# Moving the adaLN loads and the spill and mixer-row stores of a recurrence stage from SyncE's DMA queue to GpSimd's

## The chip, the cores and the metric

The kernel runs on one core of one Trainium2 chip. The metric is the device time of one execution in microseconds (us). The kernel before the change took 2364.33 us in the median of three runs (2362.54 to 2365.67). About 0.2 % (4.7 us) is what a measurement of this kernel can tell from no change.

## The reference

One decoder block on x (512 tokens x 2048 channels, float32), modulated by a vector c:

```python
c_act = silu(c)
mod = c_act @ w_ada + b_ada                  # 6 x 2048: shift, scale, gate, twice
h = rmsnorm(x, norm1_g) * (1 + sc1) + sh1
p = h @ w_in                                 # r, k, v, three low-rank inputs, pool channels
y_rwkv = rwkv7_mixer(p[..., :N_RWKV_COLS])   # 16 heads of 64: a recurrence over 512 tokens
y_pool = pool_mixer(p[..., N_RWKV_COLS:])    # causal means over windows 2, 4, 8, 16
x = x + gt1 * (concat([y_rwkv, y_pool]) @ w_out)
h = rmsnorm(x, norm2_g) * (1 + sc2) + sh2
x = x + gt2 * conv_ffn(h)                    # up 2048 -> 2 x 5632, conv of width 3, gate, down
out = rmsnorm(x, norm_f_g)
```

The recurrence of one head holds a 64 x 64 state `S` and does, for every token, `S = S * w + (S a) b^T + v k^T; y = S r`. Everything is float32.

## The kernel before, in words

Activations lie transposed, channels on the 128 partitions and the 512 tokens on the free axis. A float32 product of full accuracy is made of three TensorE matmuls (`mm3`, lines 120 to 122) on a high and a low part of weights and activations. Weights come as tiles of 128 x 512: `split_weights` (line 111) loads one into `wraw` (4 buffers) on SyncE's queue (SP), ScalarE makes the high part `whi` (line 113), VectorE the low part `wlo` (line 115).

The program has four stretches: the first norm with the first eight columns of the input projection (up to about 180 us in the profile); the recurrence stage, which this change is about (to about 750 us); the output projection; and the gated MLP (from about 980 us to the end).

The recurrence stage works on eight pairs of heads, p = 0 to 7. For each pair:

- `win_pair(p)` makes the three projection tiles r, k, v of the pair (16 x 3 matmuls of 128x512 each). ScalarE and VectorE apply the token shift (lines 233, 234), and line 615 stores each tile from `spill` (2 buffers) to DRAM (`sp`). `start_pair` loads it again later (line 623).
- `stage_a(p)` makes decays and keys, and the lower-triangular blocks `nt` (line 420). The 16 x 16 corners of the blocks are inverted on VectorE with 64 partitions: `nt` goes to DRAM (`dn`, line 423, four DMAs), comes back in another layout (`nl`, line 427, two DMAs), is solved by 14 steps of two small VectorE operations (lines 435 and 437, between lines 429 and 438), goes to DRAM (`dxz`, line 443, four DMAs), and comes back as `x4l` (line 446, four DMAs). These are the round trips.
- `stage_b(p)` builds the inverse of the whole block out of the corners with small matmuls, from line 474 to line 519.
- `stage_c(p)` goes over four chunks of 128 tokens with the state (lines 532 to 582), normalises, multiplies by the gate (line 604) and stores the mixer row to DRAM (`mixd`, line 605).
- `ada_rest` takes 28 of the 192 pieces of the rest of the adaLN product: a load of 128 x 512 into `war` (3 buffers, line 350), and on VectorE a multiply-accumulate with the broadcast `cq` (line 351), whose sum is read out by a second instruction of the same line. Nothing needs these sums before the recurrence has ended.

Loops are unrolled, and a scheduler decides the order: it takes the instructions with their priorities (`stage_a`, `stage_b` and `stage_c` are of high priority, projections and `ada_rest` fill in), estimates when each could run, and writes one fixed order for each engine. On the chip every engine and every DMA queue works through its own order and waits with all that stands behind when the next instruction's semaphores are not there yet. A load into `war` waits until VectorE has ended the multiply-accumulate three pieces earlier; a weight load waits until `wlo` four tiles earlier is made; a store waits for the tile that it stores.

Of the kernel before, what the change touches and what calls it, by code (L numbers as in the profile page):

```python
# [55 lines left out]
def block_kernel(ctx, tc, a, out, stop=None, dbg=None):  # L56
    nc = tc.nc
    V, S, G, PE = nc.vector, nc.scalar, nc.gpsimd, nc.tensor
# [112 lines left out]
    mixd = [tc.dram_tile([P, T], F32, name=f"mixd{i}") for i in range(16)]  # L171
# [5 lines left out]
    if True:  # L177
# [28 lines left out]
        for k in range(KT):  # L206
            for part in (1, 0):
                j = part * 16 + k
                wa = p0.tile([P, D], F32, tag="wa", name="wa", bufs=4)
# [21 lines left out]
        if True:  # L231
            def shift(ps, m, dst):
                S.activation(dst, ps, AF.Copy, scale=drv[:, m : m + 1])
                V.scalar_tensor_tensor(dst[:, 1:T], ps[:, 0 : T - 1], col("mu", m), dst[:, 1:T],
                                       op0=ALU.mult, op1=ALU.add)

            def ring(name):
                return ring16(name)[:, 16:]
# [14 lines left out]
            def vtile(name):  # L253
                return ra.tile([P, T], F32, tag="v", name=name, bufs=2)

            rkv0 = []
            for i, m in ((3, 0), (4, 8), (5, 16)):
                t = vtile("v") if i == 5 else ring("rkv")
# [64 lines left out]
    def win_tile(fi):  # L323
        ps = mmtile()
        project(ps, a["win1"][fi - 8, :, :], H)
        return ps
# [16 lines left out]
    def ada_rest(n0, n1):  # L343
        for n in range(n0, n1):
            kq, j = divmod(n, 48)
            if j == 0:
                cq[0] = ra.tile([P, T], F32, tag="cq", name="cq")
                nc.sync.dma_start(cq[0], cact[0:1, kq * T : (kq + 1) * T].partition_broadcast(P))
            wa = ra.tile([P, T], F32, tag="war", name="war", bufs=3)
            nc.sync.dma_start(wa, a["ada2"][kq, j, :, :])  # L350
            V.scalar_tensor_tensor(wa, wa, 1.0, cq[0], op0=ALU.mult, op1=ALU.mult,
                                   accum_out=modq[:, kq, j : j + 1])

# [169 lines left out]
    def stage_c(p, q):  # L523
# [71 lines left out]
        rs = ra.tile([P, T], F32, tag="post", name="rs", bufs=2)  # L595
# [6 lines left out]
        PE.matmul(pg, q.lw[:, 1, :], xg1, start=True, stop=False)  # L602
        PE.matmul(pg, q.lw[0:32, 2, :], xg2[0:32, :], start=False, stop=True)
        V.tensor_mul(rs, rs, pg)
        nc.sync.dma_start(mixd[p], rs)

    sp = {}

    def win_pair(p):
        for i in range(3):  # L610
            ps = win_tile(8 + 3 * (p - 1) + i)
            t = ra.tile([P, T], F32, tag="spill", name="spill", bufs=2)
            shift(ps, 8 * i + p, t)
            d = tc.dram_tile([P, T], F32, name=f"sp{p}_{i}")
            nc.sync.dma_start(d, t)
            sp[p, i] = d

    def start_pair(p):
# [14 lines left out]
    with hp():  # L633
        q = start_pair(0)
        stage_b(0, q)
    win_pair(1)
    for p in range(NP):
        if p + 1 < NP:
            if p + 2 < NP:
                win_pair(p + 2)  # L640
            with hp():
                qn = start_pair(p + 1)
        with hp():
            stage_c(p, q)
            if p + 1 < NP:
                stage_b(p + 1, qn)
                q = qn
        ada_rest(min(28 * p, 192), min(28 * p + 28, 192))
# [69 lines left out]
    def quad(i, name, dt=F32):  # L718
        return rb.tile([P, 4, T], dt, tag=f"x2_{i}", name=name)
# [37 lines left out]
    for k0 in range(4, KT, 4):  # L757
# [4 lines left out]
        for f in range(8):  # L762
            out_block(f, k0)
            if k0 == 8 and f % 2:
                t = quad(f // 2, "x2")
# [227 lines left out]
    for n, j in enumerate(order):  # L993
        wa, wb = wq[2 * (n % 2)], wq[2 * (n % 2) + 1]
# [169 lines left out]
    rs = Slot("rs")  # L1164
# [102 lines left out]
```

## Time and profile before

| | |
|---|---|
| median of three runs | 2364.33 us (2362.54 to 2365.67) |
| the profiled execution | 2367.32 us, its span 2365.6 us |
| mean granted TensorE clock | 0.989 |
| TensorE matmul busy | 2259.0 us (95 %) |
| VectorE busy | 1637.7 us (69 %) |
| ScalarE busy | 1066.4 us (45 %) |
| GpSimd busy | 126.2 us (5 %), nothing between about 195 and 860 us |
| DMA queue of SP (q1) | 413.21 MB, 54.5 % of the 16 engines |
| DMA queue of GpSimd (q0) | 66.07 MB, 13.6 % |

The profile is of one execution, so its rows are set against its own 2367.32 us. An engine is called busy while an instruction runs; the ends of matmuls are modelled, so the idle time of TensorE is a lower bound on what it loses. A row of waits says which engine waited at which line, for whom, how long in total, how often and the longest; SPq is SP's DMA queue, POOL is GpSimd, PE is TensorE, DVE is VectorE, ACT is ScalarE.

### The profile page before, as it was taken

The numbers are of one execution on the slowest core, as the hardware profiler recorded it, in microseconds if no ns is written. First come the engines' busy times: TensorE is split into PE (matmuls) and PEld (weight loads), VectorE is DVE, ScalarE is ACT, GpSimd is POOL, SyncE is SP. The second block draws the span as 40 slices with busy tenths as digits, with TensorE's granted clock in tenths as the row PEclk, the third lists the DMA queues.
The fourth block names the chain that finished last, engine by engine and source line by source line (L and its number), as shares of the span: only waits on it lengthen the run. The fifth ranks groups of instructions, "written<-read, shape, count | busy, mean of one in ns | idle before, by whom it ended". The sixth has DMA issues, their size and how long they took to land.

```text
span 2365.6 us, 42857 instructions
## 1 busy us (share of the span) xinstructions
PE 2259.0 (95%) x17122; PEld 1965.8 (83%) x17122; DVE 1637.7 (69%) x2591; ACT 1066.4 (45%) x1499; POOL 126.2 (5%) x185
## 2 busy tenths in 40 slices
PE   3879999999999999999999999999999999999997
PEld 2656666666666789999999999999999888888897
DVE  6987687777684456788888877777777645353354
ACT  3235253445433345665555555555555522233353
POOL 0000000000000000010101000000000000110000
PEclk9999999999999999999999999999999999999999
DMA  9976556566672756598888877777776767663464
GB/s 345 339 232 184 164 157 175 153 179 188 172 207 74 242 190 191 169 284 246 231 245 234 237 212 199 197 198 199 199 197 185 237 212 272 228 211 117 123 183 160
DMA packets 226234, 483.06 MB, mean 204 GB/s; under 512 B 74545, under 2 KB 79601, under 8 KB 217841
## 3 DMA queue, kind: packets, MB, share of 16 engines
q1 hardware_dynamic: 206114, 413.21, 54.5%
q0 software_dynamic: 18864, 66.07, 13.6%
q8 instruction: 134, 2.20, 0.4%
q10 hardware_dynamic: 1056, 1.05, 0.1%
q14 instruction: 66, 0.54, 0.1%
HBM read 441.70 MB, written 38.54 MB: 203 GB/s over the span
## 4 chain that ended last, share of the span: by engine, by line
PE 57%; issue 8%; DVE 1%; DMA 1%; ACT 1%; POOL 0%; POOLq 0%; DVEq 0%; ACTq 0%
PE b L122 18%; PE b L120 18%; PE b L121 18%; DMA wrow<-wup 1%; PE mm L122 1%; PE mm L121 1%; PE mm L120 1%; PE pb L122 0%; PE pa L122 0%; PE pa L120 0%; PE pa L121 0%; PE pb L120 0%; PE pb L121 0%; ACT x L787 0%; PE pa L298 0%
## 5 line engine op out<-in xcount | busy, mean ns | idle before, releaser
L122 PE MATMUL b<-t,ulo 128*128 128x256 f32 x1408 | 397.2, 282 | 0.0
L120 PE MATMUL b<-t,uhi 128*128 128x256 f32 x1408 | 396.8, 282 | 0.0
L121 PE MATMUL b<-t,uhi 128*128 128x256 f32 x1408 | 396.7, 282 | 0.0
L122 PE MATMUL b<-act,ulo 128*128 128x512 f32 (+1 forms) x880 | 308.0, 350 | 0.0
L121 PE MATMUL b<-act,uhi 128*128 128x512 f32 (+1 forms) x880 | 307.8, 350 | 0.0
L120 PE MATMUL b<-act,uhi 128*128 128x512 f32 (+1 forms) x880 | 307.7, 350 | 0.0
L120 PE MATMUL b<-y,uhi 128*128 128x256 f32 x1056 | 297.4, 282 | 2.7 <-ACT uhi L854 2.7
L122 PE MATMUL b<-y,ulo 128*128 128x256 f32 x1056 | 297.3, 282 | 0.5 <-DVE ulo L856 0.5
L121 PE MATMUL b<-y,uhi 128*128 128x256 f32 x1056 | 297.1, 281 | 0.0
L856 DVE TENSOR_TENSOR ulo<-wd,uhi 128x1024 fp32r<-128x1024 f32 (+1 forms) x120 | 136.3, 1136 | 217.9 <-ACT uhi L854 213.0
L113 ACT CAST whi<-wraw 128x512 fp32r<-128x512 f32 x236 | 145.5, 620 | 274.7 <-PE mm L121 115.3
L120 PEld LDWEIGHTS b<-t,uhi 128*128 128x128 f32 x1408 | 266.9, 190 | 0.0
L122 PEld LDWEIGHTS b<-t,ulo 128*128 128x128 f32 x1408 | 266.9, 190 | 0.0
L121 PEld LDWEIGHTS b<-t,uhi 128*128 128x128 f32 x1408 | 266.8, 190 | 0.0
L854 ACT CAST uhi<-wquart 128x1024 fp32r<-128x1024 f32 x156 | 164.0, 1052 | 202.6 <-PE b L121 176.2
L854 ACT CAST uhi<-wd 128x1024 fp32r<-128x1024 f32 (+1 forms) x120 | 117.6, 980 | 293.2 <-PE b L121 291.1
L856 DVE TENSOR_TENSOR ulo<-wquart,uhi 128x1024 fp32r<-128x1024 f32 x156 | 190.9, 1224 | 72.0 <-ACT uhi L854 72.0
L115 DVE TENSOR_TENSOR wlo<-wraw,whi 128x512 fp32r<-128x512 f32 x236 | 161.1, 688 | 100.3 <-ACT whi L113 92.6
L854 ACT CAST uhi<-r 128x1024 fp32r<-128x1024 f32 x132 | 138.8, 1051 | 163.2 <-PE b L121 161.3
L856 DVE TENSOR_TENSOR ulo<-r,uhi 128x1024 fp32r<-128x1024 f32 x132 | 161.3, 1222 | 61.9 <-ACT uhi L854 61.9
L120 PEld LDWEIGHTS b<-y,uhi 128*128 128x128 f32 x1056 | 199.6, 189 | 3.1 <-ACT uhi L854 3.1
L122 PEld LDWEIGHTS b<-y,ulo 128*128 128x128 f32 x1056 | 199.3, 189 | 0.9 <-DVE ulo L856 0.9
(314 smaller groups left out, 4719.0 us busy)
## 6 DMA issues: line engine op xcount, KB each, us to landing
wquart<-wup SPq DMA_DIRECT2D x176, 512.0 KB, 4.8
wa<-ada SPq DMA_DIRECT2D x48, 1024.0 KB, 6.9
war<-ada SPq DMA_DIRECT2D x192, 256.0 KB, 3.4
wd<-wdn SPq DMA_DIRECT2D x80, 512.0 KB, 3.8
wraw<-win SPq DMA_DIRECT2D x140, 256.0 KB, 4.1
wraw<-wout SPq DMA_DIRECT2D x96, 256.0 KB, 3.5
wquart<-wup POOLq DMA_DIRECT2D x44, 512.0 KB, 7.5
r<-wup SPq DMA_DIRECT2D x44, 512.0 KB, 4.6
```

The source lines that it names most:

```text
L113: S.copy(hi, raw)
L115: eng.tensor_tensor(lo, raw, hi[:, :].bitcast(F32), op=ALU.subtract)
L120: PE.matmul(ps, wh, xh, start=start, stop=False, skip_group_check=more)
L121: PE.matmul(ps, wh, xl, start=False, stop=False, skip_group_check=more)
L122: return PE.matmul(ps, wl, xh, start=False, stop=stop, skip_group_check=more)
L854: S.copy(hi[:, 0:n], src)
L856: lo_of[0] = V.tensor_tensor(lo[:, 0:n], src, hi[:, 0:n].bitcast(F32), op=ALU.subtract)
```

## The change

The issue of three kinds of DMA moves from SP to GpSimd (`G` is `nc.gpsimd`): the 192 loads of `war`, the 21 stores of projection tiles and the 8 stores of mixer rows. Weight loads, the round trips (`dn`, `nl`, `dxz`, `x4l`), the loads of `rkv` and `v` from `sp`, of `lw` and of `cq`, and the pool rows stay on SP. No computation changes.

```diff
@@ ada_rest
             wa = ra.tile([P, T], F32, tag="war", name="war", bufs=3)
-            nc.sync.dma_start(wa, a["ada2"][kq, j, :, :])
+            G.dma_start(wa, a["ada2"][kq, j, :, :])
             V.scalar_tensor_tensor(wa, wa, 1.0, cq[0], op0=ALU.mult, op1=ALU.mult,
                                    accum_out=modq[:, kq, j : j + 1])
@@ stage_c
         V.tensor_mul(rs, rs, pg)
-        nc.sync.dma_start(mixd[p], rs)
+        G.dma_start(mixd[p], rs)
@@ win_pair
             d = tc.dram_tile([P, T], F32, name=f"sp{p}_{i}")
-            nc.sync.dma_start(d, t)
+            G.dma_start(d, t)
             sp[p, i] = d
```

Since the scheduler estimates the two queues anew, the order changes on all engines of the recurrence stage. On SP, around the round trip of the last pair (`dn_6395` is its `dn`, `sp_2_5790` its v tile, `dxz_1094` its solved corners), there stands before:

```order
L350 DMA war<-ada 128x512
L423 DMA dn_6395<-nt 32x8x32
L623 DMA v<-sp_2_5790 128x512
L423 DMA dn_6395<-nt 32x8x32 x3
L350 DMA war<-ada 128x512 x3
L427 DMA nl<-dn_6395 32x16x16 x2
L350 DMA war<-ada 128x512 x3
L111 DMA wraw<-win 128x512 x2
L350 DMA war<-ada 128x512 x3
```

and now:

```order
L423 DMA dn_6395<-nt 32x8x32 x2
L623 DMA v<-sp_2_5790 128x512
L423 DMA dn_6395<-nt 32x8x32 x2
L427 DMA nl<-dn_6395 32x16x16 x2
L111 DMA wraw<-win 128x512
L443 DMA dxz_1094<-xyl 32x16x16 x4
L111 DMA wraw<-win 128x512
L446 DMA x4l<-dxz_1094 32x16x32 x4
```

The loads of `war` are gone from between the DMAs of the round trip; one weight load stands between some of them.

On GpSimd, whose queue had nothing between its first memsets and line 771, there now stands, from the store of the fourth mixer row (`mixd_103`) to the last load of `war`, this (`sp_0_4072` to `sp_2_4228` are the projection tiles of pair 5, `sp_0_4854` and `sp_1_4932` two of pair 6):

```order
L605 DMA mixd_103<-rs 128x512
L615 DMA sp_0_4072<-spill 128x512
L350 DMA war<-ada 128x512 x9
L615 DMA sp_1_4150<-spill 128x512
L350 DMA war<-ada 128x512 x9
L615 DMA sp_2_4228<-spill 128x512
L350 DMA war<-ada 128x512 x17
L605 DMA mixd_104<-rs 128x512
L350 DMA war<-ada 128x512 x3
L615 DMA sp_0_4854<-spill 128x512
L350 DMA war<-ada 128x512 x7
L615 DMA sp_1_4932<-spill 128x512
```

After that no load of `war` is left. In the order of before, 127 of the 192 loads stood ahead of the store of `mixd_104` and the last ones behind that of `mixd_106`; now 182 stand ahead of `mixd_104`, and all 192 ahead of `sp_1_4932`.

On VectorE, the start of the solve of the last pair (lines 429 to 437; the rows between belong to the chunks of pair 6 and to fillers) read before:

```order
L429 TENSOR_TENSOR xyl<-nl,lanei 64x256
L542 TENSOR_TENSOR L<-pb,masks 128x768
L435 TENSOR_TENSOR prod<-xyl,nl 64x14
L573 SCALAR_TENSOR_TENSOR sbd_1085<-ch,fdec,sf 64x64
L437 TENSOR_TENSOR xyl<-xyl,prod 64x14
L573 SCALAR_TENSOR_TENSOR sbd_1085<-ch,fdec,sf 64x64
L435 TENSOR_TENSOR prod<-xyl,nl 64x26
L351 SCALAR_TENSOR_TENSOR war,modq<-war,cq 128x512
L437 TENSOR_TENSOR xyl<-xyl,prod 64x2x13
L351 SCALAR_TENSOR_TENSOR war,modq<-war,cq 128x512
L435 TENSOR_TENSOR prod<-xyl,nl 64x36
L351 SCALAR_TENSOR_TENSOR war,modq<-war,cq 128x512
```

and reads now:

```order
L429 TENSOR_TENSOR xyl<-nl,lanei 64x256
L573 SCALAR_TENSOR_TENSOR sbd_1085<-ch,fdec,sf 64x64
L435 TENSOR_TENSOR prod<-xyl,nl 64x14
L573 SCALAR_TENSOR_TENSOR sbd_1085<-ch,fdec,sf 64x64
L437 TENSOR_TENSOR xyl<-xyl,prod 64x14
L542 TENSOR_TENSOR L<-pb,masks 128x768
L435 TENSOR_TENSOR prod<-xyl,nl 64x26
L437 TENSOR_TENSOR xyl<-xyl,prod 64x2x13
L435 TENSOR_TENSOR prod<-xyl,nl 64x36
L115 TENSOR_TENSOR wlo<-wraw,whi 128x512
L437 TENSOR_TENSOR xyl<-xyl,prod 64x3x12
L435 TENSOR_TENSOR prod<-xyl,nl 64x44
```

Between lines 429 and 438 of the eight solves the order of before has 3, 0, 12, 10, 7, 11, 7 and 14 multiply-accumulates of line 351, the order of now 9, 13, 10, 11, 11, 13, 0 and 0. TensorE's rows of the stage are the same matmuls, mixed in another order; its order from the output projection on is unchanged.

## The prediction

> **What bounds the kernel now.** I read the page first, for the engine on which the end hangs.
>
> ```profile
> PE 2259.0 (95%) x17122; PEld 1965.8 (83%) x17122; DVE 1637.7 (69%) x2591; ACT 1066.4 (45%) x1499; POOL 126.2 (5%) x185
> PE 57%; issue 8%; DVE 1%; DMA 1%; ACT 1%; POOL 0%; POOLq 0%; DVEq 0%; ACTq 0%
> ```
>
> The chain that ended last is TensorE's, and a DMA has 1 % of it. A change of queues moves the end only where it makes TensorE wait more or less. So I next read the busy time of each engine in stretches (columns: PE, PEld, DVE, ACT, POOL busy with counts, granted clock, DMA share, GB/s).
>
> ```profile
> 200.00:400.00 200.00, 191.48 (x1908) 134.43 (x1906) 150.82 (x394) 82.83 (x129) 0.00 (x0) 0.98 0.59 165
> 400.00:600.00 200.00, 195.68 (x2019) 135.23 (x2018) 154.85 (x403) 93.56 (x142) 0.00 (x0) 0.99 0.61 171
> 600.00:750.00 150.00, 141.57 (x1349) 97.58 (x1349) 100.50 (x257) 57.27 (x91) 0.00 (x0) 0.99 0.56 159
> 750.00:860.00 110.00, 108.82 (x462) 86.28 (x462) 50.59 (x82) 43.31 (x69) 2.34 (x4) 1.00 0.62 201
> ```
>
> The first three rows are the recurrence. TensorE is idle there for 8.5 + 4.3 + 8.4 = 21.3 us. That is the purse of every gain: fillers that a faster recurrence no longer needs run later at the same price, as the fourth row shows (1.2 us idle in 110). VectorE is busy 406.2 of 550 us (74 %), so 143.8 us of it are free. The DMA engines are about 60 % busy; their bandwidth is not what runs out.
>
> Then the waits, from 190 to 760 us: those of SP's queue, and behind the dots those of the engines.
>
> ```profile
> SPq L350 <- DVE war L351: 62.4, 57, 6.4
> SPq L615 <- DVE spill L234: 43.1, 10, 10.8
> SPq L350 <- DVE xyl L437: 28.9, 27, 3.4
> SPq L350 <- DVE prod L435: 28.7, 27, 4.4
> SPq L605 <- DVE rs L604: 15.8, 5, 9.3
> ...
> DVE U L559 <- PE ch L557: 22.7, 21, 2.6
> DVE wlo L115 <- ACT whi L113: 22.6, 21, 4.4
> DVE war L351 <- DMA war<-ada: 17.0, 17, 3.4
> ACT whi L113 <- DMA wraw<-win: 16.6, 4, 9.3
> ACT sq L397 <- DMA rkv<-sp: 7.1, 3, 4.4
> ```
>
> SP's queue stands 62.4 + 28.9 + 28.7 + 43.1 + 15.8 = 178.9 us at the three kinds of DMA that move, with weights and round trips behind them. What the engines feel of DMAs is much less: 17.0 us VectorE for `war`, 16.6 and 7.1 us ScalarE for weights and for `rkv`. No long wait of TensorE itself is on a DMA. SP's blocked time is mostly spent ahead of need.
>
> **The change part by part.**
>
> *The moved issues.* Their landings on SP, from the DMA part of the page, and what loads and stores of the same 256 KB take on GpSimd's queue elsewhere in this run:
>
> ```profile
> war<-ada SPq DMA_DIRECT2D x192, 256.0 KB, 3.4
> sp<-spill SPq DMA_DIRECT2D x21, 256.0 KB, 2.3
> mixd<-rs SPq DMA_DIRECT2D x8, 256.0 KB, 2.3
> x<-x2d POOLq DMA_DIRECT2D x16, 256.0 KB, 6.7
> x2d<-x POOLq DMA_DIRECT2D x8, 256.0 KB, 3.4
> ...
> L1123 POOL DMA_DIRECT2D yd<-yd x12: 539/539/539, 2100.9 to 2165.3; - x12
> ...
> DMA to landing us min/median/max: 2.8/3.9/5.6
> ```
>
> The last two rows are the tile `yd` from 2100 to 2170 us: spaced loads, as `war` will be (one store is among them). 3.9 against 3.4: a `war` load lands 0.5 us later. The ends are 0 (the minimum of 2.8 lies under SP's median) and 3.3 us (the 6.7 of `x2d`, sixteen loads issued in one burst). I take 0.5, the row nearest in spacing. The Trainium skill ("DMA: Bandwidth & Descriptors", section "Latency and other measured facts") gives about 0.6 us to the first byte on SyncE's path and about 1 us on GpSimd's; by its 0.4 the load term below would be 7 instead of 9 us. The stores land 1.1 us later by the same rows (3.4 against 2.3). Nothing feels that: `rkv` loads stand well behind, `mixd` is read only after the recurrence, and a `spill` buffer comes back after two projection tiles. I cost the stores at 0; without that cover they would cost up to 29 x 1.1 = 32 us. GpSimd's own issue is 0.54 us each, 221 x 0.54 = 119 us on an engine that had nothing to do there: 0.
>
> *What a later load costs VectorE.* These are the multiply-accumulates of 190 to 860 us and their accumulator reads:
>
> ```profile
> L351 DVE SCALAR_TENSOR_TENSOR war<-war,cq 128x512 f32<-128x512 f32 x179 | 120.3, 683 | 17.4 <-DMA war<-ada 17.0
> L351 DVE DVE_READ_ACCUMULATOR war<-war,cq 128x1 f32 x179 | 14.5, 81 | 0.0
> ```
>
> One piece costs 0.683 + 0.081 = 0.76 us. With three buffers a load starts when the piece three back has ended, so VectorE has to have landing time's worth of other work between. I went through the 192 loads and pieces in the timeline, with each load's landing and the end of the VectorE instruction ahead. With every load issued as soon as its buffer is free, VectorE waits 12.2 us; with 0.5 us more to land 24.7 us, with 1.0 us more 43. That is 12.5 us more for the old order. The new order is denser: 182 instead of 127 pieces ahead of the fifth mixer row, so 12.5 x 182 / 127 = 18 us. Ahead of line 351 VectorE is in order, so the solve's next step, `wlo` and the chunk's `U` stand behind a late piece. Between all of it reaching TensorE (18) and none (0) I take half, **+9 us**: half of the pieces stand inside the solves, on the chain, the others in time that is free.
>
> *The denser order itself.* The fifth mixer row is ready here:
>
> ```profile
> 539.63 0.67 DVE L604 TENSOR_TENSOR rs<-rs,ch 128x512 f32<-128x512 f32 x1
> ```
>
> 55 more pieces by the fifth mixer row are 55 x 0.76 = 42 us more VectorE work. The free time from 200 us to there is 49.2 us of the first stretch and 0.7 x 45.2 of the second, 81 us. It fits, but the solves of pairs 0, 1, 3, 4 and 5 get longer by 1 to 13 pieces. This is one chain of a pair that I can see in full (`x4l` here is the fourth leg of the round trip):
>
> ```profile
> 415.59 1.92 SPq L446 DMA_DIRECT2D x4l<-dxz  x4
> 424.33 0.61 ACT L449 COPY x<-x4l 128x512 f32<-128x512 f32 x1
> ...
> x4l<-dxz SPq DMA_DIRECT2D x32, 64.0 KB, 3.0
> ```
>
> The four issues end at 417.5 and land 3.0 us later, and the copy runs at 424.3, so this chain has about 4 us of play at its end, and a delay of one pair is taken up before TensorE's order feels it. Bounds: 0, and half of 42. I take **+4 us**, a fifth of the upper end.
>
> *The free tail.* Pairs 6 and 7 have no pieces left; their solves lose 7 + 14 pieces, 16 us of VectorE work. TensorE's idle time in their stretch is 8.4 us. I let half of it go: **-4 us** (ends 0 and -8.4).
>
> *SP relieved.* Around one `dn`-`nl` hop SP did this:
>
> ```profile
> 377.84 1.82 SPq L423 DMA_DIRECT2D dn<-nt  x4
> 381.03 0.35 SPq L350 DMA_DIRECT2D war<-ada  x1
> 382.56 0.35 SPq L111 DMA_DIRECT2D wraw<-win  x1
> 383.17 0.33 SPq L350 DMA_DIRECT2D war<-ada  x1
> 383.98 0.86 SPq L427 DMA_DIRECT2D nl<-dn  x2
> ...
> 224.18 1.42 SPq L423 DMA_DIRECT2D dn<-nt  x3
> ...
> 233.41 1.02 SPq L427 DMA_DIRECT2D nl<-dn  x2
> ...
> dn<-nt SPq DMA_DIRECT2D x32, 32.0 KB, 2.1
> ```
>
> `dn` had landed by about 379.2 + 2.1 = 381.3 (the last of four issues, 1.82 us long in all); `nl` went out at 384.0, held up 2.7 us by two `war` loads and a weight. The weight stays in front in the new order of most pairs. Read so, with each DMA's own landing, the eight holds are 0.1 to 5.9 us (the largest is the pair at 224 us) and 13.6 in all, 1.7 a pair, inside the play above. What TensorE feels is the purse's part that follows `rkv` and weights: I take **-3 us**, between 0 and the whole 21.3.
>
> *Sum:* 9 + 4 - 4 - 3 = **+6 us**. On the profiled execution 2367.3 + 6 = 2373.3. That execution is 3.0 us over the median of 2364.33, so I predict **2370 us**, 0.25 % slower.
>
> **The rivals.**
>
> *A: the loads starve VectorE.* If GpSimd's landings look like the burst (6.7 us), three buffers give one piece per (6.7 + 0.76) / 3 = 2.5 us. The new order asks for 182 pieces by 540 us less the 13 ahead of 190 (192 less the 179 counted above), 169 in 350 us, one per 2.1 us, so loads and not VectorE set the pace: 169 x 0.42 = 71 us late, half of it on TensorE as above, 35, and the denser order's 4: about **+40 us**, 2404. It decides from about 3 x 2.1 - 0.76 = 5.5 us of landing on. For it: `war` and the weights now share the DMA engines from two queues, and GpSimd's queue is in order too, so a load stands behind a `mixd` or `sp` store that waits for its tile (15.8 and 43.1 us of such waits). Against it: spaced loads took 3.9. The same page of the Trainium skill (section "SWDGE vs HWDGE vs iDMA") says that GpSimd writes its descriptors into SBUF state that VectorE's fast two-port mode locks it out of; by that its issue would stretch beside a busy VectorE, which would strengthen this rival. The twelve issues beside VectorE took 539 ns each, without any stretch, so the trace does not bear it out.
>
> *B: faster, since SP was the hidden clock.* The mechanism: blocked SP delays weights and `rkv`, and those are TensorE's long waits. Its price is half of the purse for SP (-10.6) with the late loads costing nothing (landing as on SP), and the tail's -4 lies in that purse: **-10 us**, 2354. It decides where extra landing is under about 0.2 us. For it: 178.9 us of blocked queue, a 9.3 us gap of ScalarE on one weight. Against it: the sum of what engines felt (16.6 + 7.1 us in seven waits) is small and lies on ScalarE, which is busy under half of the time.
>
> *C: nothing arrives.* TensorE has fillers everywhere and each pair has play; gains and losses stay under it: 0 us, 2364. The Trainium skill's same page (section "Issuing engines are not separate DMA queues") states that transfers issued from several engines run on the same 16 DMA engines and that spreading them saves only issue time, which speaks for this. For it, from rows: the DMA engines are at 60 %, and TensorE idles 21.3 of 550 us. Against it: the scheduler rewrote the whole stage, and a rewritten order rarely costs exactly the same.
>
> **How the numbers follow.** My case (between +2 and +20 us) has 0.40; A 0.15; B 0.28; C 0.17. Under +4.7 us, the 0.2 % that a measurement of this kernel can tell from no change, fall a small part of my case (0.06) and most of C (0.14, the rest of it slower). That gives faster 0.28, same 0.20, slower 0.52. The range leaves out the outer half of A and a little of B: from 2351 (-13) to 2400 (+36). My own case alone is 2366 to 2384.
>
> **What would show it.** Right: `war` on GpSimd's queue at 3.7 to 4.3 us to landing; VectorE's wait for `war` at 30 to 45 us, all ahead of 560 us; no multiply-accumulate after about 560; SP's waits at lines 350, 615 and 605 gone; TensorE's idle time from 200 to 600 us up from 12.8 to 20 to 30 us, from 600 to 750 down to about 4. Wrong: landings over 5.5 us with VectorE's waits above 80 (A); VectorE's wait for `war` not above 17 and TensorE's idle time under 15 us over the stage (B); idle time unchanged in every stretch (C). If the stretch from 860 us on differs by more than 3 us, the cause lies outside all of these, since the order there is the same.

## The result, and the profile after

The changed kernel took 2426.60 us in the median of four runs (2417.22 to 2431.99), the kernel before 2363.87 us beside it: 1.0256 times as long, with a 95 % interval from 1.0239 to 1.0274. That is 62.7 us slower, where I had forecast 6. The profiled execution took 2417.22 us, with a span of 2415.5 us and a mean clock of 0.981 (0.989 before), so it explains 49.9 us of the difference.

First the page's line of busy time, then the windows of the same stretches as before (columns: PE, PEld, DVE, ACT, POOL busy with counts, granted clock, DMA share, GB/s), all of the changed kernel:

```profile
PE 2270.4 (94%) x17122; PEld 1971.9 (82%) x17122; DVE 1639.7 (68%) x2591; ACT 1062.3 (44%) x1497; POOL 244.9 (10%) x406
200.00:400.00 200.00, 176.95 (x1769) 124.41 (x1765) 155.01 (x412) 77.17 (x118) 50.07 (x93) 0.96 0.68 189
400.00:600.00 200.00, 179.00 (x1596) 121.73 (x1595) 148.24 (x410) 80.19 (x123) 52.21 (x97) 0.94 0.65 188
600.00:750.00 150.00, 137.38 (x1532) 96.06 (x1534) 85.62 (x195) 59.11 (x91) 5.41 (x10) 0.95 0.32 84
750.00:860.00 110.00, 109.07 (x640) 79.06 (x635) 47.77 (x89) 38.93 (x65) 0.54 (x1) 1.00 0.40 126
860.00:2300.00 1440.00, 1431.19 (x10237) 1348.60 (x10235) 976.48 (x1148) 684.94 (x926) 120.05 (x170) 1.00 0.72 210
```

TensorE idles 23.1 + 21.0 + 12.6 = 56.7 us from 200 to 750 us, 35.4 more than before. The same 17122 matmuls take 2270.4 instead of 2259.0 us, 11.4 more, and the clock in the three stretches is 0.94 to 0.96 where it was 0.98 to 0.99. The two together are 46.8 of the 49.9 us. After 860 us TensorE idles 8.8 us; the same window of before has 1431.66 us busy, 8.3 us idle. So nearly all of the loss is in the recurrence.

Next the engines' waits of the changed kernel from 190 to 800 us (engine, line, who is waited for: us in total, times, longest), and behind the dots, to set beside them, the multiply-accumulate's group from 190 to 860 us:

```profile
DVE war L351 <- DMA war<-ada: 47.1, 48, 3.6
ACT sq L397 <- DMA rkv<-sp: 20.8, 4, 8.9
PE pb L483 <- DVE Tm L477: 20.7, 5, 7.0
PE pb L474 <- ACT x L449: 6.8, 3, 3.6
ACT x L449 <- DMA x4l<-dxz: 6.4, 2, 3.8
...
L351 DVE SCALAR_TENSOR_TENSOR war<-war,cq 128x512 f32<-128x512 f32 x178 | 119.8, 683 | 52.3 <-DMA war<-ada 47.1 <-DMA cq<-cact 4.8
```

VectorE waits for `war` 48 times in place of 17. ScalarE waits 20.8 us for `rkv`, the projection tiles that come back from DRAM, in place of 7.1. TensorE has two waits that were not among the long ones before: for `Tm`, which VectorE makes, and for `x`, which ScalarE copies from the end of the round trip. So now the DMAs' landings, of the changed kernel from 190 to 760 us (KB each, median us to landing):

```profile
war<-ada POOLq DMA_DIRECT2D x176, 256.0 KB, 3.5
x4l<-dxz SPq DMA_DIRECT2D x32, 64.0 KB, 6.0
dn<-nt SPq DMA_DIRECT2D x32, 32.0 KB, 2.5
dxz<-xyl SPq DMA_DIRECT2D x32, 32.0 KB, 3.7
...
dxz<-xyl SPq DMA_DIRECT2D x32, 32.0 KB, 2.7
```

The row behind the dots is `dxz` of before. `war` itself lands nearly as fast as on SP. What slowed is `x4l`, which the change did not touch: 3.0 us before, 6.0 now. `dxz` went from 2.7 to 3.7. The changed kernel holds its own comparison: the `x4l` of the first six pairs, beside which loads of `war` run, took 5.3 to 7.2 us (median 6.5), those of the last two, after the last load at 601.9 us, 2.4 to 3.2 (median 2.8).

### The profile page after: what moved, and what is told of

It reads as the page before. It is cut to its first block, busy times and chain, and to the rows that moved or that the text cites. A ratio compares the mean times of both kernels' runs of the same rounds, so it can differ in the third digit from the quotient of the medians.

```text
span 2415.5 us, 42943 instructions
## 1 busy us (share of the span) xinstructions
PE 2270.4 (94%) x17122; PEld 1971.9 (82%) x17122; DVE 1639.7 (68%) x2591; ACT 1062.3 (44%) x1497; POOL 244.9 (10%) x406
## 4 chain that ended last, share of the span: by engine, by line
PE 63%; issue 20%; DVE 7%; DMA 4%; POOL 3%; ACT 3%; SPq 0%; POOLq 0%; DVEq 0%; ACTq 0%
PE b L122 17%; PE b L120 17%; PE b L121 17%; DVE jk L212 3%; POOL war L350 2%; PE mm L120 2%; PE mm L121 2%; PE mm L122 2%; DMA war<-ada 1%; DMA wrow<-wup 1%; DMA sp<-spill 1%; DMA wraw<-win 0%; PE pb L541 0%; PE pa L298 0%; DVE wlo L115 0%
## 5 line engine op out<-in xcount | busy, mean ns | idle before, releaser
L122 PE MATMUL mm<-ah,wlo 128*128 128x512 f32 x464 | 195.6, 422 | 5.7 <-DVE wlo L115 5.7
```

The costliest lines, as they stand in the source:

```text
L122: return PE.matmul(ps, wl, xh, start=False, stop=stop, skip_group_check=more)
```

## The experiments

The change did two things: three kinds of DMA go through another queue, and the scheduler wrote another order for every engine. To separate them, I add a function that is called once the program is traced. It ties each instruction of TensorE, VectorE and ScalarE to the one ahead of it in a list, with a dependency that the scheduler sees and that leaves no semaphore on the chip. These three engines then issue in the list's order; SP and GpSimd stay with the scheduler, so in the runs that mix an order with other queues these two have orders of their own. "Old order" and "new order" below mean the lists of the kernel before and of the changed one. Ratios are to the kernel before, run beside each; the interval in brackets is of 95 %.

### Queue or order?

My theory was ORDER, the rewritten order; the rivals SHARE, transfers of two queues that slow each other whatever the order, and WAIT, loads that come too late for VectorE. The changed kernel with the old order:

```diff
 # the changed kernel
+    fix_order(tc)        # lists of the kernel before
```

> The 29 stores and 192 loads go out on GpSimd's queue as in the change, but TensorE, VectorE and ScalarE are held to the order of the kernel before. Three theories of the 62 us lost. ORDER (the rewritten, denser order is what costs): back to within 8 us of before. SHARE (GpSimd's 256 KB transfers slow the small DMAs of the round trips, x4l from 3.0 to 6.0 us to landing): most of the loss stays, 35 to 55 us slower than before, x4l at 5 to 6 us. WAIT (loads on GpSimd come too late for VectorE, which is in order): 15 to 30 us slower, VectorE's wait for war at 25 to 35 us instead of 17.

2373.32 us, 1.0049 (1.0031 to 1.0068): some 12 us (7 to 16), where ORDER allows 8, and far from the 35 to 55 of SHARE. And the other half, all DMAs on SP with the new order:

```diff
 # the kernel before
+    fix_order(tc)        # lists of the changed kernel
```

> All DMAs stay on SP, but TensorE, VectorE and ScalarE are held to the order of the changed kernel. ORDER: 45 to 65 us slower than before. SHARE: within 10 us of before, x4l at about 3 us. WAIT: 20 to 40 us slower, since the denser order has to wait for loads from SP too, the more so as SP's queue holds loads back behind other DMAs.

2458.56 us, 1.0417 (1.0394 to 1.0440): 98 us, more than any of the three had said. The four corners, of which 1 and 1.0256 are the two kernels themselves:

| | old order | new order |
|---|---|---|
| all on SP | 1 | 1.0417 |
| three kinds on GpSimd | 1.0049 | 1.0256 |

Without the new order the loss is not there; the queues alone cost 0.5 %. In the new order GpSimd's queue even helps by 1.6 %. The engines' waits show the difference, for the kernel with all on SP in the new order and, behind the dots, for that on both queues in the old order:

```profile
DVE war L351 <- DMA war<-ada: 90.6, 41, 9.6
PE pb L474 <- ACT x L449: 11.0, 2, 8.5
...
ACT x L449 <- DMA x4l<-dxz: 21.0, 4, 11.7
DVE war L351 <- DMA war<-ada: 19.9, 21, 2.5
```

In SP's queue the loads of the denser order stand behind all else, and VectorE waits up to 9.6 us for one, although they land in 3.5 us once issued. In the old order, the same loads through GpSimd's queue cost VectorE 19.9 us, hardly more than the 17.0 of before. ScalarE's wait for `x4l` grew there from 2.1 to 21.0 us, but it is not the price: in the old order it is 16.9 us with the stores alone on GpSimd, and that kernel is as fast as the one before (below).

### Loads or stores?

Each kind moved alone, with the scheduler free:

```diff
 # the kernel before
-            nc.sync.dma_start(wa, a["ada2"][kq, j, :, :])
+            G.dma_start(wa, a["ada2"][kq, j, :, :])
```

> Only the 192 loads go to GpSimd, the 29 stores stay on SP; the scheduler orders anew. SHARE and WAIT: nearly the whole loss, 45 to 65 us slower. A fourth theory, FIFO (a load stands behind a store on GpSimd's queue that waits for its tile, 89.6 + 94.0 us of such waits in the changed kernel): only 15 to 30 us slower, as the loads never stand behind a store.

2415.99 us, 1.0238 (1.0213 to 1.0262): nearly all of the loss. FIFO falls, and so does the thought that the stores come late behind the loads: ScalarE waits 8.7 us for `rkv` here, in place of 20.8, and the time is nearly the same.

```diff
 # the kernel before
-        nc.sync.dma_start(mixd[p], rs)
+        G.dma_start(mixd[p], rs)
-            nc.sync.dma_start(d, t)
+            G.dma_start(d, t)
```

> Only the 29 stores go to GpSimd, the 192 loads stay on SP; the scheduler orders anew. SHARE: within 8 us of before (7 MB instead of 57 MB on the second queue), x4l at 3 to 3.5 us. WAIT: within 8 us of before, or up to 10 us faster, as SP no longer waits 43 + 16 us at the stores. ORDER: open, as this order is a third one; within 20 us either way.

2375.0 us, 1.0063 (1.0039 to 1.0087). Both again, with `fix_order(tc)` and the lists of the kernel before:

> Order of the kernel before; only the 192 loads on GpSimd. With both moved the old order gave 12 us over before. If the loads' sharing with the round trips is that cost: 8 to 14 us slower, x4l at 3.5 us. If the stores are (rkv waits 12.8 us instead of 7.1): within 4 us of before, or up to 4 us faster as SP is freed.

2370.09 us, 1.0024 (1.0008 to 1.0039). That is some 6 us, between the two forecasts.

> Order of the kernel before; only the 29 stores on GpSimd. If the stores' later landing is what the old order loses with both moved (rkv waits 12.8 us instead of 7.1): 6 to 12 us slower. If the loads are: within 4 us of before.

2365.45 us, 1.0006 (0.9991 to 1.0021). The stores on GpSimd's queue cost nothing that can be measured once the order is held, as the prediction had it; the 0.6 % of the free run is again an order's. The loads cost 0.24 %. The two add up to 0.3 where both together gave 0.5, which the intervals allow.

### What in the new order costs the time?

The new order brings the multiply-accumulates forward. Three things come with that: their own work on VectorE (WORK), their loads (LATE), and new places for everything else (PLACE). The kernels from here to the last run leave out parts of the computation; they are for their time alone. First the loads go, and the multiply-accumulates stay:

```diff
 # the changed kernel, fix_order with its own lists
-            G.dma_start(wa, a["ada2"][kq, j, :, :])
-            V.scalar_tensor_tensor(wa, wa, 1.0, cq[0], ...
+            V.scalar_tensor_tensor(wa, cq[0], 1.0, cq[0], ...
```

> Queues and order of the changed kernel, but the 192 loads of war are left out: VectorE's multiply-accumulates read cq instead and cost the same. The order is what costs 62 us; three theories of how. LATE (the denser order asks for pieces faster than three buffers can be filled, and VectorE, which is in order, waits 47 us): within 10 us of before, either way. WORK (55 more pieces ahead of the fifth mixer row stretch the chains of the first pairs by their own duration): still 40 to 60 us slower. PLACE (the rest of the order, fitted to round trips that the scheduler takes to be faster than they are): still 30 to 60 us slower.

2371.95 us, 1.0037 (1.0022 to 1.0052). Then their work goes too:

```diff
+            V.scalar_tensor_tensor(wa[:, 0:8], cq[0][:, 0:8], 1.0, cq[0][:, 0:8], ...
```

> As the kernel without loads, and the multiply-accumulates work on 8 columns instead of 512, so that they cost about 0.07 + 0.08 us instead of 0.68 + 0.08 us. LATE: as without loads, within 10 us of before, or a few us faster. WORK: within 10 us of before, and 40 us or more faster than the kernel without loads. PLACE: still 30 us or more slower than before.

2370.97 us, 1.0036 (1.0019 to 1.0053). The windows from 200 to 600 us of the two, first with the full work and behind the dots with the short:

```profile
200.00:400.00 200.00, 191.07 (x1953) 133.68 (x1952) 168.72 (x471) 81.83 (x129) 5.42 (x10) 0.98 0.34 85
400.00:600.00 200.00, 186.17 (x1864) 128.95 (x1862) 155.03 (x401) 89.58 (x134) 5.96 (x11) 0.97 0.33 85
...
200.00:400.00 200.00, 192.03 (x1964) 135.94 (x1964) 123.10 (x474) 81.82 (x130) 5.42 (x10) 0.98 0.34 84
400.00:600.00 200.00, 187.60 (x1900) 130.31 (x1898) 117.16 (x405) 90.09 (x136) 5.96 (x11) 0.97 0.33 83
```

VectorE's third column falls by 83 us in 400, and TensorE's first gains 2.4. WORK is refuted: the pieces brought forward are free as far as VectorE's time goes. PLACE is at most the 0.4 % that is left. What costs is the loads: without its 192 loads the new order loses almost nothing. Whether they cost by coming late, these two runs do not say. The same cut in the old order on SP, as a control:

```diff
 # the kernel before, fix_order with its own lists
-            nc.sync.dma_start(wa, a["ada2"][kq, j, :, :])
-            V.scalar_tensor_tensor(wa, wa, 1.0, cq[0], ...
+            V.scalar_tensor_tensor(wa, cq[0], 1.0, cq[0], ...
```

> Queues and order of the kernel before, the loads of war left out (the multiply-accumulates read cq). What the loads cost before: with 17 us of VectorE waiting and 120 us of SP's queue blocked by them, LATE expects 0 to 8 us faster than before, since TensorE idles 21 us over the whole stage. If blocked weights and round trips had been the hidden clock, 10 us or more faster.

2354.52 us, 0.9956 (0.9940 to 0.9972). So the loads cost 10 us in the old order on SP, and about 52 in the new one on GpSimd's queue (1.0256 less 1.0037). The 10 us lie at the edge of the second forecast, the hidden clock. This run takes away the bytes and the blocking together; the loads moved off SP in the old order gained nothing (1.0024), which speaks against the blocking.

### VectorE's waits, or the bytes?

A late load can cost through VectorE, which stands at line 351, or through the DMA engines that it shares with the round trips. Five buffers in place of three let the loads run ahead. They need room, which `xg2` and `cq` give up; a control does the same with three.

```diff
 # the changed kernel, fix_order with its own lists; the control has bufs=3
-            xg2 = ra.tile([P, T], F32, tag="xg2", name="xg2")
+            xg2 = ra.tile([P, T], F32, tag="post", name="xg2", bufs=2)
-        t = ra.tile([P, T], F32, tag="war", name="pw", bufs=3) if gi < 3 else ring("pw")
+        t = ra.tile([P, T], F32, tag="war", name="pw", bufs=5) if gi < 3 else ring("pw")
-                cq[0] = ra.tile([P, T], F32, tag="cq", name="cq")
-                nc.sync.dma_start(cq[0], cact[0:1, kq * T : (kq + 1) * T].partition_broadcast(P))
-            wa = ra.tile([P, T], F32, tag="war", name="war", bufs=3)
+                cq[0] = xwa
+            wa = ra.tile([P, T], F32, tag="war", name="war", bufs=5)
-        PE.matmul(pg, q.lw[0:32, 2, :], xg2[0:32, :], start=False, stop=True)
+        PE.matmul(pg, q.lw[0:32, 2, :], xg1[0:32, :], start=False, stop=True)
```

> Queues and order of the changed kernel with five buffers of war instead of three. To make room xg2 and cq are left out: the gate's second product reads xg1, and the multiply-accumulates multiply by xwa; the instructions of the engines stay the same. LATE: VectorE's wait for war falls from 47 to under 15 us, and the time to 5 to 25 us over before. WORK and PLACE: 40 us or more slower than before whatever the wait.

> The control of the kernel with five buffers: the same parts left out, three buffers. All theories: 50 to 65 us slower than before, VectorE's wait for war 40 to 55 us, as in the changed kernel.

Five buffers: 2400.98 us, 1.0155 (1.0122 to 1.0188). Three: 2421.32 us, 1.0251 (1.0213 to 1.0290). VectorE's wait, TensorE's for `Tm` and the landings from 190 to 800 us, with five buffers and behind the dots with three:

```profile
DVE war L350 <- DMA war<-ada: 4.5, 5, 1.6
PE pb L482 <- DVE Tm L476: 3.9, 4, 1.8
war<-ada POOLq DMA_DIRECT2D x172, 256.0 KB, 4.0
x4l<-dxz SPq DMA_DIRECT2D x32, 64.0 KB, 5.6
...
DVE war L350 <- DMA war<-ada: 52.9, 51, 3.9
PE pb L482 <- DVE Tm L476: 17.6, 5, 6.1
x4l<-dxz SPq DMA_DIRECT2D x32, 64.0 KB, 5.9
```

VectorE's waits are nearly gone and with them 1.0 % (0.0251 less 0.0155, about 20 us between the medians; by the two intervals 0.5 more or less). TensorE's wait for `Tm`, which stands behind them on VectorE, is 13.7 us shorter. But LATE had said 5 to 25 us over the kernel before, and about 37 are left: more than half of the loss is still there, and `x4l` is nearly as slow as in the changed kernel. The last run keeps the five buffers, the count of loads, their issues and semaphores, and takes away seven eighths of their bytes:

```diff
 # the kernel with five buffers
-            G.dma_start(wa, a["ada2"][kq, j, :, :])
-            V.scalar_tensor_tensor(wa, wa, 1.0, cq[0], ...
+            G.dma_start(wa[:, 0:64], a["ada2"][kq, j, :, 0:64])
+            V.scalar_tensor_tensor(wa[:, 0:64], wa[:, 0:64], 1.0, cq[0][:, 0:64], ...
```

> As the five-buffer kernel in the changed kernel's order and queues (xg2 and cq left out as there: the gate's second product reads xg1, the multiply-accumulate multiplies by xwa), and each of the 192 loads of war brings only the first 64 of 512 columns, 32 KB in place of 256 KB; the multiply-accumulate runs on these 64 columns. The count of loads, their issues on GpSimd, their buffers and their semaphores stay. With five buffers VectorE hardly waited for war (4.5 us), and yet that kernel was 1.0155 of the kernel before, where the one without loads was at 1.0037. SHARE (what is left is the bytes of the loads, which slow x4l and the other round trips of the solves on the DMA engines): about 1.004 (1.001 to 1.007), x4l lands in 3.3 to 3.8 us, TensorE idles about 26 us from 200 to 750 us. ISSUE (what is left comes with the loads as instructions, whatever their size: GpSimd's issues, waits and semaphores): about 1.0155 (1.012 to 1.019), idle about 41 us. Between the two both have a part.

2365.66 us, 1.0013 (0.9998 to 1.0027): SHARE, and ISSUE falls. Its windows and landings from 200 and 190 us on, with GpSimd as busy as in the changed kernel:

```profile
200.00:400.00 200.00, 191.87 (x1960) 134.91 (x1960) 128.47 (x480) 81.97 (x130) 55.32 (x104) 0.98 0.41 98
400.00:600.00 200.00, 188.75 (x1869) 131.15 (x1867) 117.96 (x394) 89.55 (x135) 46.57 (x88) 0.95 0.39 96
600.00:750.00 150.00, 146.24 (x1421) 99.02 (x1420) 77.96 (x173) 60.50 (x96) 3.24 (x6) 1.00 0.27 69
...
war<-ada POOLq DMA_DIRECT2D x171, 32.0 KB, 2.7
dxz<-xyl SPq DMA_DIRECT2D x32, 32.0 KB, 2.5
dn<-nt SPq DMA_DIRECT2D x32, 32.0 KB, 2.6
x4l<-dxz SPq DMA_DIRECT2D x32, 64.0 KB, 3.2
```

TensorE idles 23.1 us over the three stretches, as in the kernel before (21.3), where the five-buffer kernel idles 41.1 (186.03, 178.54 and 144.36 us busy). The profiled execution is the slowest of its ten, 10.5 us over the median. The round trips are fast again. The run shortens the multiply-accumulate as well, which the pair of runs without loads showed to be free there.

So the bytes cost the time. By what way they reach TensorE is less clear. With five buffers and full loads `dn` took 3.1, `dxz` 3.6 and `x4l` 5.6 us; the differences are 0.5 + 1.1 + 2.4 = 4.0 us a pair, 32 us over eight pairs, and the medians of the two kernels are 35.3 us apart. That looks like the whole account, but the trace does not bear it out. From the first issue of `dn` to the start of the copy `x`, the eight chains add up to 365.1 us with full loads and 348.7 with small ones, 16.4 apart, and 11.4 of these lie in the solves, between the transfers. Most of what the landings lost was play. Another way is `rkv`, which also goes to DRAM and back; the waits from 190 to 800 us, with full loads and behind the dots with small ones:

```profile
ACT sq L396 <- DMA rkv<-sp: 24.9, 5, 10.9
DVE ar L451 <- DMA rkv<-sp: 11.8, 3, 8.0
ACT x L448 <- DMA x4l<-dxz: 6.3, 2, 4.3
...
ACT sq L396 <- DMA rkv<-sp: 12.7, 5, 4.6
DVE ar L451 <- DMA rkv<-sp: 4.7, 2, 2.6
```

The waits for `rkv` fell by 19.3 us, that for `x4l` by 6.3. No run separates the two ways. With the loads alone moved, in an order of its own, ScalarE waited only 8.7 us for `rkv` and the loss was nearly whole, so this wait is not needed for it.

The multiplication ahead of the mixer row's store tells how far each recurrence was delayed. The rows are of before, after, five buffers and small loads, in this order, with the first and the last start:

```profile
L604 DVE TENSOR_TENSOR rs<-rs,ch x8: 668/684/689, 297.4 to 754.1; 128x512 f32<-128x512 f32 x8
...
L604 DVE TENSOR_TENSOR rs<-rs,ch x8: 669/684/689, 311.9 to 791.1; 128x512 f32<-128x512 f32 x8
...
L603 DVE TENSOR_TENSOR rs<-rs,ch x8: 669/686/689, 301.3 to 775.0; 128x512 f32<-128x512 f32 x8
...
L603 DVE TENSOR_TENSOR rs<-rs,ch x8: 669/687/689, 292.2 to 746.6; 128x512 f32<-128x512 f32 x8
```

With small loads the last row comes 7.5 us sooner than before, and the kernel is no faster, so a start is not the kernel's time. Of the 2.56 %, then, about 1.0 is VectorE's waiting for loads, about 1.4 the loads' bytes beside SP's transfers of the recurrence (0.0155 less 0.0013), and what is left is within what can be measured. No kernel here beats the one before with the whole computation; the nearest, the stores alone in the old order, equals it.

## Why the prediction was wrong, point by point

The sign was right and the size was not: +6 us forecast, +62.7 measured, outside the range.

- **The denser order itself** is the step that failed. It priced the pieces brought forward by VectorE's time alone, found that it fits, and took +4 us with 21 as the upper end. The work did fit: cutting it to 8 columns changed nothing (1.0037 and 1.0036). But each piece brings a load of 256 KB to the same place, and the term has no price for these bytes. The prediction had read a mean DMA share of 60 % as room ("their bandwidth is not what runs out"). The share rose only from 0.59 and 0.61 to 0.68 and 0.65, yet beside the loads `x4l` took twice as long to land, and the waits for `rkv` grew. That is the larger part, about 1.4 %.
- **A delay of one pair is taken up before TensorE's order feels it**: in part. Most of what the landings lost to the bytes was play, as the run with small loads shows; the rest was not. I read 4 us of play in one chain of one pair. By the landings in the trace the eight pairs of before have 0.1 to 5.0 us between the last landing of `x4l` and the copy, and the pair that I read has the most. In the new order TensorE waits 6.8 us for `x`, the copy of `x4l`, and 20.7 for `Tm`.
- **What a later load costs VectorE**, +9 us: `war` landed 0.2 us later (3.6 against 3.4 over the run), not 0.5, yet VectorE's wait rose by 30.1 us, not 18. Scaling 12.5 by 182/127 took the pieces as evenly spread; in the new order they stand closer. The five buffers, which took the wait to 4.5 us while `war` landed in 4.0 us, show that it was the spacing and not the landing. The half that was to reach TensorE was about right: removing 48 us of wait returned about 20 us of time. So the term was too small because the wait was: by that share the 30.1 us more cost some 13 us (an estimate), where the term has 9. The 1.0 % counts the waits that the kernel before had as well. The Trainium skill ("DMA: Bandwidth & Descriptors", section "Latency and other measured facts") would have the first byte 0.4 us later; the landings of `war` moved by 0.2.
- **The free tail**: right in its mechanism. The solve of the last pair, from line 429 to line 438, takes 23.5 us in before (two rows ahead of the dots) and 11.3 in after:

```profile
667.15 0.41 DVE L429 TENSOR_TENSOR xyl<-nl,lanei 64x256 f32<-64x256 f32 x1
690.27 0.38 DVE L438 COPY xyl<-xyl 64x256 f32<-64x256 f32 x1
...
718.00 0.42 DVE L429 TENSOR_TENSOR xyl<-nl,lanei 64x256 f32<-64x256 f32 x1
728.90 0.36 DVE L438 COPY xyl<-xyl 64x256 f32<-64x256 f32 x1
```

  It is already in the +37.0 us of the last mixer row (791.1 less 754.1). TensorE's idle time from 600 to 750 us did not fall to 4 but rose to 12.6.
- **SP relieved**, -3 us, and with it **rival B**: in the old order moving the three kinds costs 0.5 %, so nothing was to be gained there. In the new order it is worth 1.6 %, as the table of four corners shows. Its sign hangs on the order.
- **The stores at 0**: right (1.0006 in the old order). **The stretch from 860 us on**: right, 0.5 us of difference in idle time.
- **Rival A** came near in its price (+40 us) for half a reason. It wanted landings of 5.5 us or more, and they were 3.6. That loads share the DMA engines from two queues was in its argument, for the weights; what slowed were the round trips, and `wraw` landed as before (4.1 us in both). That its price came near is luck.
- **Rival C**'s rule (the Trainium skill, the same page, section "Issuing engines are not separate DMA queues": transfers from several engines run on the same 16 DMA engines) agrees with the trace, since `x4l` on SP took 6.0 us beside dense loads on GpSimd's queue and 3.2 beside small ones. The conclusion "nothing arrives" did not follow from it: sharing was the cost, not a reason for none.
- **What would show it** named 20 to 30 us of idle time from 200 to 600 us, and 44.1 came; 30 to 45 us of waits, and 47.1 came; no multiply-accumulate after 560, and the last began at 607.6, since everything was late. `war` landed in 3.5 us, under the 3.7 to 4.3. Longer matmuls (11.4 us, beside a lower granted clock) were in no step.

## What to carry to other kernels

When a DMA changes its queue under a scheduler, two changes arrive, the queue and a rewritten order; hold the order and measure each, before a cost is put on either. Price a filler that moves forward by all that it brings, its load above all: if the work fits into free time, the bytes may still slow the transfers that the critical chain waits for, and a mean DMA share does not show it. A buffer count that covered a landing in one order need not cover it in the next.

## What the hardware showed that I had not expected

A small transfer's landing can double though it stays on its queue. `x4l`, 64 KB, took 3.0 us with all on SP, 3.5 with the three kinds on GpSimd in the old order, and 6.0 in the new one; with all on SP in the same new order it took 2.9. These are medians, and single pairs differ: in the old order on two queues the last pair's four took 6.4 to 8.0. The Trainium skill's sentence that DMAs of several queues share the engines (cited above) allows this, but gives no price for it. The trace does, for the pair whose hop the prediction shows. The DMA queues' lines (packets, MB, share of 16 engines) from the first issue of its `x4l` to the last landing, 415.6 to 419.3 us in before and behind the dots 431.7 to 439.6 in after:

```profile
q1 hardware_dynamic: 2256, 0.46, 66.9%
...
q0 software_dynamic: 313, 1.03, 52.8%
q1 hardware_dynamic: 2391, 0.71, 42.6%
```

The DMA engines are busy for over 95 % of the second, where the mean share from 400 to 600 us is 0.65. GpSimd's packets had 52.8 % of 7.9 us, 4.2 us, and 7.9 less 3.7 is 4.2 as well. Over the first six pairs the same stretches add up to 27.3 us in before and 46.4 in after, and GpSimd's packets had 44 % of the latter, 20 us. The pages' queue lines, of before and behind the dots of after, show how the packets differ:

```profile
q1 hardware_dynamic: 206114, 413.21, 54.5%
q0 software_dynamic: 18864, 66.07, 13.6%
...
q1 hardware_dynamic: 174290, 355.26, 45.8%
q0 software_dynamic: 36544, 124.02, 20.9%
```

The same 57.95 MB are 31824 packets on SP's queue, 1.8 KB each, and 17680 on GpSimd's, 3.3 KB each. In the window of before, 2128 of the 2256 packets were under 512 B, those of `x4l` among them. Whether the size of GpSimd's packets matters beside their bytes, no run isolates.
